# Sums of squares for the token norms: a GpSimd running sum in place of a TensorE product per row

## The chip, the cores and the metric

The kernel runs on one core of one Trainium2 chip. The metric is the device time of one execution in microseconds (us); the figure that counts is the median of several runs. One core has five engines with a queue each: TensorE (PE in the profile, its weight loads PEld), VectorE (DVE), ScalarE (ACT), GpSimd (POOL) and SyncE (SP), which here only starts DMAs. TensorE writes to PSUM, the others work mostly on SBUF.

## The reference

Two layers over 256 latent tokens and 256 context tokens of width 1024. What matters here is the norm that stands ahead of each mixer and of each mixture of experts:

```
def rms_norm(x, gain):
    xf = x.astype(jnp.float32)
    y = xf * lax.rsqrt(jnp.mean(xf * xf, axis=-1, keepdims=True) + NORM_EPS)
    return (y * gain.astype(jnp.float32)).astype(x.dtype)

for layer in range(DEPTH):
    hx = modulate(rms_norm(x, norm_mix[layer]), shift, scale)     # and hc from ctx
    ...                                                           # four mixers
    x = x + gate * (mixed @ w_out[layer])
    hx2 = modulate(rms_norm(x, norm_ffn[layer]), shift, scale)
    x = x + gate * hierarchical_moe(hx2, ...)                     # 16 experts, 2 of them per token
```

In layer 0 both streams are carried on; in layer 1 only the latent tokens are, so its second norm is over 256 tokens. All arithmetic is float32. For each token the mean of 1024 squares is needed: four times in the kernel (layer 0 mixers, layer 0 experts, layer 1 mixers, layer 1 experts).

## The kernel before, in words

The residual stream X is held in SBUF with features on partitions: eight "rows" j = 0..7 of 128 features, and for each row a tile of 128 partitions x 256 tokens per stream s (s = 0 latent, s = 1 context). A row is final once its last residual update has been added. Then `Rms.row(j)` (L349) takes over: for each stream ScalarE writes the squares into a 256-wide work tile (tag "t", six buffers), and TensorE multiplies them by `mean32`, 128 x 32 numbers of 1/1024, into one of four 32-partition strips of a PSUM bank (L354). A product in float32 stands in the trace as two records. `Rms.end` (L356) copies each bank to SBUF (ACT, tile name t<-ss), adds the four strips with products by `sel1`, one per 128 tokens (PE, ssb<-cb,t), takes the root (ACT, rtok<-ssb), inverts it (DVE), and broadcasts it back over the partitions (PE L370, then ACT rstd<-ssb). The norm proper (L377) multiplies X by rstd.

`Rms` is made and fed in four places:
- at the start of the kernel for X as loaded (L1548), two streams;
- in `out_proj` (L1000): four groups g of weight columns, each 48 products into two PSUM banks (tile pw, three buffers); then VectorE adds the rows j = 2g and 2g + 1 to X (L1020, one instruction per row and stream), and `sums.row(j)` follows at once. In layer 0 there are two streams, in layer 1 one, and there also a 32-column router product per row (tile rt);
- in the last `scatter` of layer 0's experts (L1397, called at L1486): for each row j four products (tile sct) into one of three PSUM banks, one VectorE addition per stream (L1407), `sums.row(j)`. This scatter stands behind a conditional block (L1438) that is not taken; two work tiles of tag "t" hold the placement matrices Pm until it ends.

Work that fills in around these places: the modulation products (tile ada), which run while a norm is computed, and `split_w`, which splits weights into two parts (tile wsp): a ScalarE copy, then half of the subtraction on VectorE and half on GpSimd. Weights come in 1 MB pieces through SP's queue into 22 shared slots; a DMA starts when an earlier user has given its slot back. The framework's scheduler fixes the order in each engine's queue ahead of time, by priority and its own estimates; each engine then works strictly in that order.

Helpers record most operations at one line: every product is L152, every ScalarE operation L155, every two-input elementwise operation L158, so rows of the trace are told apart by tile names.

Of the kernel before, what the change touches and what calls it, by code (L numbers as in the profile page):

```python
# [15 lines left out]
AF = mybir.ActivationFunctionType  # L16
OP = mybir.AluOpType
# [98 lines left out]
def build(tc, xT, cT, vec, cst, ada, w_in, w_out, wg, wu, wd, outT, es, dbg=None):  # L116
    nc = tc.nc
    dbg = dbg or {}
    V, S, G, T = nc.vector, nc.scalar, nc.gpsimd, nc.tensor
# [8 lines left out]
    def nm(s):  # L128
        cnt[0] += 1
        return f"{s}_{cnt[0]}"  # L130
# [6 lines left out]
    def ps(tag, shape=(512,), name="ps"):  # L137
        return psp.tile([128] + list(shape), F32, name=nm(name), tag=tag, bufs=PSB[tag])
# [3 lines left out]
    def wt(shape, tag, dt=F32, bufs=None):  # L142
        if tag in TB:
            return wk.tile([128, 516], dt, name=nm(tag), tag=tag, bufs=TB[tag])[:, :shape[0]]
        return wk.tile([128] + list(shape), dt, name=nm(tag), tag=tag, **({"bufs": bufs} if bufs else {}))
# [5 lines left out]
    def mm(out, lhsT, rhs, start, stop, **kw):  # L151
        return T.matmul(out, lhsT, rhs, start=start, stop=stop, **kw)  # L152

    def act(out, in_, f=AF.Copy, **kw):
        return S.activation(out, in_, f, **kw)  # L155

    def tt(out, a, b, op, eng=V):
        return eng.tensor_tensor(out, a, b, op=op)  # L158
# [9 lines left out]
    def load_x():  # L168
        t = [sl([8, 256], name="X") for _ in range(2)]
        for s in range(2):  # L170
            nc.sync.dma_start(t[s], xT[s])
        return lambda j, s: t[s][:, j]

    X0 = load_x()
# [5 lines left out]
    mean32 = cb[:, C_MEAN:C_MEAN + 32]  # L180
# [87 lines left out]
    def keep(n):  # L268

        live[0] = n  # L270
        issue()
# [36 lines left out]
    def ada_quad(l, q, after={}):  # L308

        pm = ps("a", name="ada")  # L310
        for k in range(KT):
            w = take('ada', l, q, k)
            M = 32 if k == 0 else 2
            for c in range(4):
                with tc.issue_after(spread[after[k]].ins) if after.get(k) in spread else nullcontext():
                    mm(pm[32 * c:32 * c + M], csil[:, k] if k else csil0[:, 0], w[:, c], k == 0, k == 7, skip_group_check=True)
            del w
            done()
            yield
        sb = wt([512], "t")  # L320
        act(sb, pm)
        pt = ps("a", name="adaT")
        for i in range(4):
            T.transpose(pt[:, 128 * i:128 * i + 128], sb[:, 128 * i:128 * i + 128], ident)
        us = slice(16 * q, 16 * q + 16)
        for s in range(2):
            tt(mods[l][:, us, s].rearrange("p (u i) -> p u i", i=4),
               pt.rearrange("p (i c r) -> p c i r", c=4, r=32)[:, :, :, s],
               (va if l + q == 0 else vs[:, l])[:, V_ADAB + 16 * q:V_ADAB + 16 * q + 16].rearrange("p (u i) -> p u i", i=4), OP.add)
        yield  # L330
# [11 lines left out]
    class Rms:  # L342


        def __init__(self, X, ns):
            self.X, self.ns = X, ns
            self.sums = [ps("m", name="ss") for _ in range(ns)]

        def row(self, j):  # L349
            g = j % 4  # L350
            for s in range(self.ns):
                sq = wt([256], "t")
                act(sq, self.X(j, s), AF.Square)
                mm(self.sums[s][32 * g:32 * g + 32, :NX], mean32, sq, j < 4, j >= 4)  # L354

        def end(self):  # L356
            n = 2 * self.ns
            pc = ps("m", [n], name="ssb")
            for s in range(self.ns):
                part = wt([256], "t")  # L360
                act(part, self.sums[s][:, :NX])
                for c in range(2):
                    mm(pc[:, 2 * s + c:2 * s + c + 1], part[:, 128 * c:128 * c + 128], sel1, s == c == 0, True,
                       skip_group_check=True)
            r = self.rtok = wt([4], "rtok", bufs=1)
            act(r[:, :n], pc, AF.Sqrt, bias=epst)
            V.reciprocal(r[:, :n], r[:, :n])
            pb = ps("m", name="ssb")
            for i in range(n):
                T.transpose(pb[:, 128 * i:128 * i + 128], r[:, i:i + 1].to_broadcast([128, 128]), ident)  # L370
            rs = []
            for s in range(self.ns):
                t = wt([256], f"rstd{s}", bufs=1)
                act(t, pb[:, NX * s:NX * s + NX])
                rs.append(t)
            return rs
# [623 lines left out]
    def out_proj(l, mh, ml, X, gate):  # L1000
        ns = 2 if l == 0 else 1
        sums = Rms(X, ns)
        sums.logits = Logits(l, X) if ns == 1 else None
        order = (2, 3, 6, 7, 0, 1, 4, 5)
        for g in range(4):
            pw = [ps("pj", name="pw") for _ in range(2)]
            hi, lo = ahead.pop(g) if g in ahead else split_w(take('out', l, g), (V, G))
            if g in AHO[l] and g < 3:
                ahead[g + 1] = split_w(take('out', l, g + 1), (V, G))
            for n_, k in enumerate(order):  # L1010
                for c in range(2):
                    cs = slice(128 * c, 128 * c + 128)
                    o = pw[c][:, :NX * ns]
                    mm(o, hi(k)[:, cs], mh(k), n_ == 0, False)
                    mm(o, hi(k)[:, cs], ml(k), False, False)
                    mm(o, lo(k)[:, cs], mh(k), False, n_ == 7)
            for c in range(2):
                j = 2 * g + c
                for s in range(ns):
                    V.scalar_tensor_tensor(X(j, s), pw[c][:, NX * s:NX * s + NX], gate[:, j, s:s + 1], X(j, s),  # L1020
                                           op0=OP.mult, op1=OP.add)
                sums.row(j)
                if sums.logits:
                    sums.logits.row(j)
        return sums
# [519 lines left out]
        plan.append(sources[key])  # L1545

    keep(LIVE[0][0])
    sums = Rms(X0, 2)  # L1548
    for j in range(8):
        sums.row(j)  # L1550
    mh, ml = mixers(0, X0, sums, first0, lambda i: (nothing(), ada_quad(0, 1), ada_quad(0, 2), nothing())[FILL[0][i]], LIVE[0])
    X = load_x()
    keep(LIVE[0][3])
    sums = out_proj(0, mh, ml, X, mods[0][:, 16:24, :])
    tap_x("x1", X)
    keep(LIVE[0][4])
    sums = moe(0, X, sums, mods[0][:, 40:48, :], ada_quad(1, 0))
# [4 lines left out]
    sums = out_proj(1, mh, ml, X, mods[1][:, 16:24, :])  # L1562
# [68 lines left out]
```

## Time and profile before

| | |
|---|---|
| median of 3 runs | 1213.12 us (1211.68 to 1213.55) |
| the profiled execution | 1214.19 us |
| its span, first to last instruction | 1212.4 us |
| PE busy | 1139.1 us, 94% |
| DVE, ACT, POOL busy | 524.8, 381.7, 189.1 us |
| from HBM | 299.29 MB |

The span is what the views cut into windows; times in them count from its start. The profiled execution lies 1.07 us above the median. In this kernel layer 0's output projection runs to about 370 us, its experts to about 697 us with the last scatter to 713 us; layer 1's output projection runs from about 929 to 963 us, its experts to the end.

### The profile page before, as it was taken

What the parts mean: (1) busy time and instruction counts of PE and PEld (TensorE: products, weight loads), DVE (VectorE), ACT (ScalarE), POOL (GpSimd) and SP (SyncE); (2) the same over time, 40 slices, a digit from 0 to 9 for tenths busy, and PEclk for the clock granted to TensorE, in tenths of its full rate; (3) what the DMA queues carried; (4) which work ended last, traced back from release to release, by engine and by line L of the source; (5) the groups of instructions that cost most, each with busy time, mean ns of one, the idle gap of its engine ahead of it and who ended that gap; (6) DMA issues with size and microseconds to landing.
All of it is one profiled execution on the core that took longest, in us unless ns stands there. A gap on an engine that the chain in (4) does not pass through costs nothing. (4 is left out here: it accounts for less than half of the span.)

```text
span 1212.4 us, 16650 instructions
## 1 busy us (share of the span) xinstructions
PE 1139.1 (94%) x6667; PEld 708.6 (58%) x6667; DVE 524.8 (43%) x1000; ACT 381.7 (31%) x648; POOL 189.1 (16%) x129
## 2 busy tenths in 40 slices
PE   5999989999998899999999789999988999999998
PEld 3699876764564453333434348975965655565654
DVE  2637658646715421322212256656887231212122
ACT  5544365533413110111000245436764221110110
POOL 1325453100302000000000012443213000000000
PEclk9999999999999899999999989999999889999999
DMA  9811016453647699898699902374245769999991
GB/s 389 330 35 70 35 36 240 177 225 123 240 177 284 273 426 426 297 387 308 211 372 426 424 7 71 139 254 163 70 174 177 288 266 402 393 388 427 425 422 39
DMA packets 44708, 303.61 MB, mean 250 GB/s; under 512 B 5456, under 2 KB 7120, under 8 KB 8784
## 3 DMA queue, kind: packets, MB, share of 16 engines
q1 hardware_dynamic: 42320, 295.52, 61.8%
q0 software_dynamic: 1296, 4.72, 1.1%
q10 hardware_dynamic: 1008, 2.22, 0.5%
q8 instruction: 56, 0.92, 0.3%
q14 instruction: 28, 0.23, 0.1%
HBM read 299.29 MB, written 3.15 MB: 249 GB/s over the span
## 5 line engine op out<-in xcount | busy, mean ns | idle before, releaser
L152 PE MATMUL pf<-hxh,wsp 128*128 128x512 f32 (+1 forms) x640 | 179.8, 365 | 9.8 <-ACT wsp L155 3.8
L152 PE MATMUL g<-w,row 128*64 128x512 f32 (+1 forms) x704 | 147.9, 595 | 2.1 <-DVE row L1335 2.1
L158 POOL TENSOR_TENSOR wsp<-w,wsp 128x1024 fp32r<-128x1024 f32 x34 | 95.1, 2800 | 334.6 <-ACT wsp L155 301.5
L152 PE MATMUL u<-w,row 128*64 128x512 f32 (+1 forms) x704 | 141.1, 592 | 0.0
L152 PE MATMUL d<-w,t 128*64 128x512 f32 (+1 forms) x704 | 137.0, 596 | 1.0 <-DVE o L1393 0.9
L152 PEld LDWEIGHTS pf<-hxh,wsp 128*128 128x128 f32 x640 | 115.2, 193 | 32.8 <-ACT wsp L155 4.7
L152 PE MATMUL pf<-hxl,wsp 128*128 128x512 f32 (+1 forms) x320 | 114.7, 360 | 1.3 <-POOL hxl L158 1.0
L152 PEld LDWEIGHTS u<-w,row 128*64 128x64 f32 (+1 forms) x704 | 55.7, 127 | 71.3 <-issue 68.9
L152 PEld LDWEIGHTS g<-w,row 128*64 128x64 f32 (+1 forms) x704 | 53.8, 127 | 74.1 <-issue 66.1
L158 DVE TENSOR_TENSOR t<-t,u 128x512 f32<-128x512 f32 x18 | 12.4, 689 | 181.9 <-PE u L152 181.9
L152 PEld LDWEIGHTS d<-w,t 128*64 128x64 f32 (+1 forms) x704 | 47.5, 126 | 73.5 <-issue 63.1
L152 PE MATMUL ptk<-wsp,hxh 128*128 128x256 f32 x480 | 90.3, 287 | 0.0
L1407 DVE SCALAR_TENSOR_TENSOR X<-sct,mods,X 128x256 f32<-128x256 f32 x112 | 50.0, 480 | 73.4 <-PE sct L152 71.5
L152 PE MATMUL sct<-t,o 128*128 128x512 f32 (+1 forms) x288 | 69.7, 368 | 10.7 <-PEq L1438 5.8
L1393 DVE SCALAR_TENSOR_TENSOR o<-d,wsl,o 128x512 fp32r<-128x512 f32 x36 | 26.3, 748 | 121.2 <-ACT o L155 120.2
L155 ACT ACTIVATE wsp<-w 128x1024 fp32r<-128x1024 f32 x72 | 73.7, 1052 | 15.9 <-POOL wsp L158 5.8
L152 PEld LDWEIGHTS ptk<-wsp,hxh 128*128 128x128 f32 x480 | 75.2, 191 | 2.3 <-issue 1.2
L152 PE MATMUL pw<-mixh,wsp 128*128 128x512 f32 (+1 forms) x256 | 67.5, 348 | 3.0 <-ACT mixh L155 3.0
L152 PEld LDWEIGHTS pf<-hxl,wsp 128*128 128x128 f32 x320 | 61.6, 193 | 11.7 <-POOL hxl L158 2.3
L152 PE MATMUL ptk<-wsp,hxl 128*128 128x256 f32 x240 | 68.2, 284 | 0.0
L152 PEld LDWEIGHTS sct<-t,o 128*128 128x128 f32 x288 | 43.9, 190 | 41.3 <-issue 26.0
L158 POOL TENSOR_TENSOR K<-K,F 64x512 f32<-64x512 f32 (+1 forms) x46 | 58.6, 1274 | 59.4 <-issue 24.1
(260 smaller groups left out, 1566.0 us busy)
## 6 DMA issues: line engine op xcount, KB each, us to landing
w<-in_wg_dram SPq DMA_DIRECT2D x64, 1024.0 KB, 8.5
w<-in_wu_dram SPq DMA_DIRECT2D x64, 1024.0 KB, 10.6
w<-in_wd_dram SPq DMA_DIRECT2D x64, 1024.0 KB, 13.1
w<-in_ada_dram SPq DMA_DIRECT2D x48, 1024.0 KB, 6.8
w<-in_w_in_dram SPq DMA_DIRECT2D x28, 1024.0 KB, 4.8
w<-in_w_out_dram SPq DMA_DIRECT2D x8, 1024.0 KB, 6.0
X<-in_xT_dram SPq DMA_DIRECT2D x4, 1024.0 KB, 4.9
hd<-hrow ACTq DMA_DIRECT2D x4, 512.0 KB, 3.6
```

What stands on the lines that cost most here:

```text
L152: return T.matmul(out, lhsT, rhs, start=start, stop=stop, **kw)
L155: return S.activation(out, in_, f, **kw)
L158: return eng.tensor_tensor(out, a, b, op=op)
L1393: V.scalar_tensor_tensor(ohl[:, 1, fs], pd[nn], w, ohl[:, 0, fs].bitcast(F32), op0=OP.mult, op1=OP.subtract)
L1407: V.scalar_tensor_tensor(X(j, s), p[:, NX * s:NX * s + NX], gate[:, j, s:s + 1], X(j, s), op0=OP.mult, op1=OP.add)
```

## The change

`Rms` gets a flag `added`, true everywhere but at the start of the kernel. With it, row 0's squares are written straight into a tile `sq[s][0]` (the buffer that later holds rstd for that stream), the squares of rows 1 to 6 are added to it by GpSimd, one addition per row and stream, and row 7's squares are kept in their own work tile. `end` multiplies both tiles by one column of `mean32`: for each stream and each 128 tokens two products accumulate in PSUM (the 128 x 128 squares are the weights, one column moves). The two PSUM banks of the strips, the copy to SBUF and the products by `sel1` fall away in the three places.

```
-    sums = Rms(X0, 2)
+    sums = Rms(X0, 2, False)
     ...
-        def __init__(self, X, ns):
-            self.X, self.ns = X, ns
-            self.sums = [ps("m", name="ss") for _ in range(ns)]
+        def __init__(self, X, ns, added=True):
+            self.X, self.ns, self.added = X, ns, added
+            if added:
+                self.sq = [[wt([256], f"rstd{s}", bufs=1)] for s in range(ns)]
+            else:
+                self.sums = [ps("m", name="ss") for _ in range(ns)]

         def row(self, j):
             g = j % 4
             for s in range(self.ns):
+                if self.added:
+                    sq = wt([256], "t") if j else self.sq[s][0]
+                    act(sq, self.X(j, s), AF.Square)
+                    if 0 < j < 7:
+                        tt(self.sq[s][0], self.sq[s][0], sq, OP.add, G)
+                    elif j:
+                        self.sq[s].append(sq)
+                    continue
                 sq = wt([256], "t")
                 act(sq, self.X(j, s), AF.Square)
                 mm(self.sums[s][32 * g:32 * g + 32, :NX], mean32, sq, j < 4, j >= 4)
     ...
             for s in range(self.ns):
+                if self.added:
+                    for c in range(2):
+                        for i in range(2):
+                            mm(pc[:, 2 * s + c:2 * s + c + 1], self.sq[s][i][:, 128 * c:128 * c + 128], mean32[:, 0:1],
+                               s == c == i == 0, True, skip_group_check=True)
+                    del self.sq[s][:]
+                    continue
                 part = wt([256], "t")
                 act(part, self.sums[s][:, :NX])
                 ...
```

## Rows read from the trace of the kernel before

**Rows 1.** Busy time by stage: window, its length, then each engine's busy us (instructions).
```profile
331.00:372.00 41.00, 41.00 (x183) 27.60 (x184) 6.30 (x16) 6.38 (x16) 0.00 (x0) 1.00 0.51 190
690.00:722.00 32.00, 22.97 (x112) 10.20 (x111) 12.48 (x28) 14.92 (x30) 4.72 (x2) 0.88 0.24 100
...
1100.00:1212.40 112.40, 102.82 (x558) 62.27 (x554) 24.96 (x53) 11.27 (x18) 0.00 (x0) 1.00 0.77 320
```

**Rows 2.** SP's waits from 960 to 1165 us: in total, times, longest.
```profile
SPq L265 <- PE d L152: 68.9, 12, 13.5
SPq L265 <- DMA w<-in_wg_dram: 3.8, 3, 1.6
```

**Rows 3.** Timeline of PE, layer 0's output projection, around one group's end.
```profile
342.27 0.61 PE L152 MATMUL pw<-mixh,wsp 128*128 128x512 f32 x2
342.72 0.39 PE L152 MATMUL pw<-mixl,wsp 128*128 128x512 f32 x1
343.04 0.62 PE L152 MATMUL ss<-t,cb 128*32 128x256 f32 x2
343.59 0.73 PE L152 MATMUL pw<-mixh,wsp 128*128 128x512 f32 x2
```

**Rows 4.** Timeline of DVE, the same projection: the additions behind groups 2, 3, 4.
```profile
342.01 1.66 DVE L1020 SCALAR_TENSOR_TENSOR X<-pw,mods,X 128x256 f32<-128x256 f32 x4 [9.69 <-PE pw L152]
355.95 1.66 DVE L1020 SCALAR_TENSOR_TENSOR X<-pw,mods,X 128x256 f32<-128x256 f32 x4 [12.27 <-PE pw L152]
369.11 1.66 DVE L1020 SCALAR_TENSOR_TENSOR X<-pw,mods,X 128x256 f32<-128x256 f32 x4 [11.50 <-PE pw L152]
```

**Rows 5.** Timeline behind that projection, from the last squares to the root.
```profile
369.62 1.65 ACT L155 ACTIVATE t<-X 128x256 f32<-128x256 f32 x4 [11.51 <-DVE X L1020]
...
373.26 0.97 PEld L152 LDWEIGHTS ssb<-cb,t 128*128 128x128 f32 x8 [0.86 <-ACT t L155]
374.36 0.26 ACT L155 ACTIVATE rtok<-ssb,epst 128x4 f32<-128x4 f32 x1 [1.46 <-PE ssb L152]
```

**Rows 6.** GpSimd's forms of two-input operation in the whole span: count, busy, mean ns.
```profile
L158 POOL TENSOR_TENSOR wsp<-w,wsp 128x1024 fp32r<-128x1024 f32 x34 | 95.1, 2800 | 334.6 <-ACT wsp L155 301.5 <-issue 22.0 <-PE sc L152 8.0
L158 POOL TENSOR_TENSOR t<-X,rstd 128x256 f32<-128x256 f32 x8 | 6.8, 875 | 47.8 <-ACT rstd L155 47.3 <-ACT H L155 0.2
```

**Rows 7.** The same operation by tile: ns least, median, most.
```profile
L158 POOL TENSOR_TENSOR t<-X,rstd x8: 730/909/1009, 376.6 to 382.9; 128x256 f32<-128x256 f32 x8
```

**Rows 8.** Timeline of layer 0's last scatter and the norm behind it.
```profile
696.98 1.62 PE L152 MATMUL sct<-t,o 128*128 128x512 f32 x3 [5.83 <-PEq L1438]
698.30 0.87 ACT L155 ACTIVATE t<-X 128x256 f32<-128x256 f32 x2 [4.26 <-DVE X L1407]
705.05 2.39 POOL L158 TENSOR_TENSOR wsp<-w,wsp 128x1024 fp32r<-128x1024 f32 x1 [8.59 <-ACT wsp L155]
...
718.22 0.26 ACT L155 ACTIVATE rtok<-ssb,epst 128x4 f32<-128x4 f32 x1 [1.87 <-PE ssb L152]
722.10 1.65 PE L152 MATMUL pf<-hxh,wsp 128*128 128x512 f32 x3 [2.64 <-ACT hxh L155]
```

**Rows 9.** Busy time of the instructions on tile ss alone, by window.
```profile
939.00:962.10 23.10, 3.27 (x12) 1.08 (x12) 0.00 (x0) 0.00 (x0) 0.93 0.68 277
```

**Rows 10.** Timeline behind layer 1's output projection.
```profile
962.68 0.81 ACT L155 ACTIVATE t<-X 128x256 f32<-128x256 f32 x2 [6.89 <-DVE X L1020]
965.33 0.26 ACT L155 ACTIVATE rtok<-ssb,epst 128x2 f32<-128x2 f32 x1 [0.42 <-PE ssb L152]
```

**Rows 11.** Busy time by stage, as rows 1; the last three columns are granted clock, DMA share, GB/s.
```profile
697.00:712.00 15.00, 15.00 (x54) 6.39 (x58) 7.77 (x15) 6.80 (x14) 2.39 (x1) 0.89 0.04 17
722.00:728.00 6.00, 5.90 (x14) 4.43 (x15) 5.33 (x11) 3.72 (x8) 2.64 (x2) 0.53 0.00 0
```

**Rows 12.** Products of the modulation between 697 and 722 us: count, then ns least, median, most.
```profile
L152 PE MATMUL ada<-w,csil x40: 592/592/617, 711.6 to 716.6; 128*2 128x512 f32 x32, 128*32 128x512 f32 x8
```

**Rows 13.** Timeline of PE at the low clock, start of layer 1's first projection.
```profile
724.12 0.63 PE L152 MATMUL pf<-hxh,wsp 128*128 128x512 f32 x1
724.54 0.63 PE L152 MATMUL pf<-hxl,wsp 128*128 128x512 f32 x1
```

## The prediction

> **What bounds the kernel now.** I read the table of busy time by stage first. Through layer 0's output projection TensorE is busy in 41.00 of 41 us, and in the last 112 us in 102.82 [rows 1]: TensorE bounds nearly everything. DMA comes close in the experts (0.77 of all engines over the last stage), so the waits of SP's queue are next: from 960 to 1165 us it waited 68.9 us for TensorE's products on d to give slots back, and 3.8 us for transfers of wg [rows 2]. The weights follow TensorE and not the other way round, so time saved on TensorE ahead of the experts moves their stream with it. The exception is the stretch from 690 to 722 us, 22.97 us busy of 32 at a granted clock of 0.88 [rows 1]: there a chain over several engines decides. Three places change: A, layer 0's output projection; B, layer 0's last scatter; C, layer 1's output projection. Each has a running part, where products of squares stand among other products, and a tail from the last square to the root.
>
> **A, running part.** Removed from it: 12 products by mean32 (the other four stand in the tail). The timeline shows what one costs beside pw: pw at 342.72, the product at 343.04, pw again at 343.59 [rows 3]. That is 0.87 us between two pw products. Undisturbed, two of them take 0.45 us, from 342.27 to 342.72 [rows 3], about 0.227 each; 48 make 10.9 us. Check it on whole groups: VectorE's additions behind groups 2, 3 and 4 start at 342.01, 355.95 and 369.11 [rows 4], so two groups take 13.94 and 13.16 us, 3.0 and 2.3 us over 10.9. In group 3 four products stand singly, which makes 0.75 us each, as the timeline shows with the stretched pw behind it; in group 4 three stand together. The first boundary has the pattern of the last, 2.3. Sum 7.6 us. In exchange there is nothing on TensorE. GpSimd's additions are hidden: it has no instruction in this stage [rows 1], and has over ten us per group for two rows. What could be late next is VectorE's release of a PSUM bank at each boundary, 0.2 to 0.3 us, so I take 7.0 (bounds 5.5 and 7.6).
>
> **A, tail.** Before: the four squares end at 369.62 + 1.65 = 371.27, then come products, a copy and the products ssb; the root starts at 374.36 [rows 5]. After: the last additions are those of row 6, whose squares end after the first and second of four, at 370.04 and 370.45. GpSimd's 128 x 256 form takes 875 ns in the mean [rows 6], between 730 and 1009 [rows 7]; the second addition ends at 371.5 to 372.1. Then four more products of N = 1 are due; today's four are 8 records in 0.97 us [rows 5], and there are eight after the change, the first stream's half during the additions. Root at 372.8 to 373.2: a gain of 1.2 to 1.6, I take 1.3. If the scheduler puts all eight behind the last addition, 0.4 is left; if an addition costs 1.9 it is a loss of about 0.7. Bounds -0.7 and 1.6.
>
> **B.** Here the scatter's 16 products by mean32 stand between sct products and pace the chain: root at 718.22, first projection product at 722.10 [rows 8], 3.9 us later. After the change GpSimd is the slowest: row 1's first square ends at 698.30 + 0.43 [rows 8], twelve additions at 0.875 + 0.05 for a handover (estimate) make 11.1, and one subtraction on wsp (2.39) may fall between them [rows 8]: 698.7 + 11.1 + 2.4 = 712.2. The last products add 1.0: root at 713.2, gain 5.0. What else stands there, two copies and a table load on ScalarE, falls away or lies under the additions. Queued behind the additions on GpSimd is that subtraction, for the layer's second column group, which is due only after the first group's products. Of the six work tiles two are held, so ScalarE's squares run at GpSimd's pace; behind them in its queue are two weight copies with the same late due time. Lower bound: additions at 1.009 with gaps of 0.08 put the root at 715.2, gain 3.0. Upper bound: additions at 0.73 without the subtraction would allow more than TensorE does. It has some 26 sct products, 8 of them at half clock at 0.42 [rows 13] and the others at 0.23, together 7.6 us, and 40 records of modulation at about 0.11 (their starts from 711.6 to 716.6 cover them with others, [rows 12]), 4.6, and 2.0 for the new products: done at 711.2, gain 7.0.
>
> **C.** Running part: the mean32 products take 3.27 us in 12 records, that is six products [rows 9], some next to router products that need the same change of shape anyway. I take 2.8 (bounds 2.0 and 3.3). Tail: squares end at 963.09 and 963.49, root at 965.33 [rows 10]. After: one addition, 963.1 to 964.0, four products of 8 records at 0.97 us, root at 965.0: gain 0.3 (bounds -0.7, addition at 1.9, and 0.7).
>
> **Sum.** 7.0 + 1.3 + 5.0 + 2.8 + 0.3 = 16.4 us off the profiled execution's 1214.19, so 1197.8; it stood 1.07 above the median, so the median is 1196.7. All lower bounds give 9.1 us (1204), all upper ones 20.2 (1193). The new order that the scheduler finds elsewhere I allow 3 us either way: own range 1190 to 1207.
>
> **Rivals.** [...]
>
> Second, the weight stream decides. If DMA and not TensorE ends the experts, time saved ahead of them is waited out there: 1213, no change. For it, DMA's share of 0.77 in the last stage [rows 1]; against it, SP's queue waits for TensorE [rows 2].
>
> Third, the other side: GpSimd's additions are far dearer than the profiled form, because each needs the result of the one two before it, a pattern that no row shows. Fifteen additions stand on a path that decides (twelve in B, two in A's tail, one in C's). At 0.93 the gain is 16.4; it is gone at 0.93 + 16.4 / 15 = 2.0 us, and at 2.8, the mean of the form four times as wide [rows 6], the kernel takes 28 us more than forecast, 1225. Against: the very form ran eight times at 1009 ns or less, beside VectorE work of the same kind [rows 7].
>
> The change could also fail to do what it says: the scheduler can put the new products, which wait for GpSimd, early in TensorE's queue, with modulation products behind them. In B that puts up to 4.6 us of modulation behind the root, hidden in part by the 3.9 us to the first projection product; 1199 to 1201, inside my range.
>
> **How the numbers follow.** Forecast (with its misordered form) 0.66; clock 0.14; weights 0.07; dear additions 0.05; more than 22 us gained, by a better order elsewhere, 0.05; an unlucky order elsewhere, about 1214 to 1217, 0.03. About 0.2% (2.4 us) is what a measurement of this kernel can tell from no change. Faster by more than that: 0.66 + 0.14 + 0.05 and a little of the weights' case, 0.87. Within it: 0.06. Slower: 0.07. The range reaches over the clock's case and both bounds: 1189 to 1208.
>
> **What would show it.** In A the additions L1020 stand 10.9 to 11.2 us apart, and no ss record is left behind the start of the kernel. GpSimd shows 12 additions of 128 x 256 in A and in B and 6 in C, at 0.73 to 1.0 us. B's root comes about 15 to 16.5 us after the first sct product behind the conditional block, against 21.2. From each norm to the next place the distances stay as before. The prediction is wrong if the additions take over 1.3 us, if sct runs at 0.42 throughout, or if TensorE waits for weights in the experts.

## Result, and the profile after

| | before | after |
|---|---|---|
| median | 1213.34 us (1211.68 to 1214.02, 4 runs) | 1199.2 us (1197.09 to 1201.26, 4 runs) |
| the profiled execution | 1214.19 us | 1197.09 us |
| its span | 1212.4 us | 1195.2 us |
| PE, DVE, ACT, POOL busy | 1139.1, 524.8, 381.7, 189.1 us | 1122.9, 526.6, 379.7, 211.6 us |

The ratio is 0.9885, with the interval 0.9864 to 0.9907: 14.1 us faster. The forecast was 1196.7, 2.5 us too low; the measured median lies inside its range of 1189 to 1208. The profiled execution of before lies above all four of its runs, that of after is the fastest of its four: the two traces differ by 17.1 us, 3 us more than the medians. So the ladder below, made from the traces, shows where the time went, and the runs of the experiments have to say how much of it is real.

The ladder takes the same event in both traces and lists after minus before; the last column is what was gained between this event and the one above it.

| event | before | after | difference | gained |
|---|---|---|---|---|
| A: addition behind the first group | 330.66 | 330.75 | +0.09 | -0.1 |
| A: addition behind the fourth group | 369.11 | 361.83 | -7.28 | 7.4 |
| A: root | 374.36 | 366.81 | -7.55 | 0.3 |
| first sct product behind the conditional block | 696.98 | 689.88 | -7.10 | -0.5 |
| B: root | 718.22 | 703.63 | -14.59 | 7.5 |
| C: addition behind the first group | 940.46 | 924.79 | -15.67 | 1.1 |
| C: addition behind the last group | 962.17 | 945.37 | -16.80 | 1.1 |
| C: root | 965.33 | 948.65 | -16.68 | -0.1 |
| layer 1's experts: first product on g | 979.01 | 962.35 | -16.66 | 0.0 |
| end of the span | 1212.4 | 1195.2 | -17.2 | 0.5 |

The stages first: busy time in windows of the kernel after, for A, for B and behind it, and for the start of C: length, busy us of PE, PEld, DVE, ACT and POOL (instructions), granted clock of TensorE, DMA share, GB/s.

```profile
331.00:363.00 32.00, 32.00 (x140) 25.55 (x138) 5.90 (x15) 5.37 (x14) 7.13 (x11) 1.00 0.61 222
690.00:704.00 14.00, 13.59 (x79) 8.31 (x79) 9.43 (x17) 9.01 (x18) 12.30 (x13) 0.86 0.05 22
704.00:708.00 4.00, 1.14 (x5) 0.74 (x5) 2.32 (x8) 1.97 (x5) 0.34 (x2) 0.52 0.00 0
708.00:712.00 4.00, 4.00 (x11) 2.95 (x12) 3.76 (x8) 2.66 (x5) 1.98 (x2) 0.63 0.00 0
...
925.00:927.00 2.00, 2.00 (x6) 0.78 (x5) 1.13 (x3) 1.25 (x3) 0.72 (x1) 0.50 1.00 418
927.00:929.00 2.00, 2.00 (x7) 1.15 (x7) 0.00 (x0) 0.00 (x0) 0.72 (x1) 0.50 0.99 418
929.00:931.00 2.00, 2.00 (x17) 2.00 (x16) 0.00 (x0) 0.00 (x0) 0.00 (x0) 0.89 1.03 426
```

A still keeps TensorE busy throughout (32.00 of 32), as in [rows 1], and GpSimd works beside it for 7.13 us, where it did nothing. B's 14 us from the skipped block to the root hold 13.59 us of TensorE and 12.30 us of GpSimd: both are nearly full. Behind the root TensorE is busy for 1.14 us of four, and the granted clock is 0.52 and 0.63 in the mean of these two stretches; [rows 11] have 0.53 from the first projection product on. The last three rows belong to C and are taken up below.

What TensorE's work gave back in A is in VectorE's additions behind groups 2, 3 and 4 (timeline of after; start, length, operation, in brackets the idle time before it and what ended it).

```profile
340.03 1.66 DVE L1039 SCALAR_TENSOR_TENSOR X<-pw,mods,X 128x256 f32<-128x256 f32 x4 [7.62 <-PE pw L152]
350.93 1.66 DVE L1039 SCALAR_TENSOR_TENSOR X<-pw,mods,X 128x256 f32<-128x256 f32 x4 [9.24 <-PE pw L152]
361.83 1.66 DVE L1039 SCALAR_TENSOR_TENSOR X<-pw,mods,X 128x256 f32<-128x256 f32 x4 [9.24 <-PE pw L152]
```

They stand 10.90 and 10.90 us apart, where [rows 4] have 13.94 and 13.16: exactly 48 undisturbed pw products of 0.227 us. The tail behind them, to the root:

```profile
362.41 1.59 ACT L155 ACTIVATE t<-X 128x256 f32<-128x256 f32 x4 [9.31 <-DVE X L1039]
362.96 1.41 POOL L158 TENSOR_TENSOR rstd<-rstd,t 128x256 f32<-128x256 f32 x2 [8.07 <-ACT t L155]
363.75 0.38 PE L152 MATMUL ssb<-cb,rstd 128*128 128x1 f32 x2 [0.30 <-POOL rstd L158]
364.06 1.06 PE L152 MATMUL ada<-w,csil 128*32 128x512 f32 x8
365.05 0.38 PE L152 MATMUL ssb<-cb,t 128*128 128x1 f32 x2
...
366.81 0.27 ACT L155 ACTIVATE rtok<-ssb,epst 128x4 f32<-128x4 f32 x1 [2.81 <-PE ssb L152]
```

The two additions end at 364.37, 2.54 us behind the start of the last VectorE addition. The root is another 2.44 us later, because eight records of modulation (ada, 1.06 us) stand between the new products in TensorE's queue, and seven of the eight new products run only behind them.

B in the timeline of after, from the skipped block to the first projection product:

```profile
689.88 7.40 PE L152 MATMUL sct<-t,o 128*128 128x512 f32 x23 [5.68 <-PEq L1457]
691.70 10.33 POOL L158 TENSOR_TENSOR rstd<-rstd,t 128x256 f32<-128x256 f32 x12 [2.24 <-ACT t L155]
697.22 4.50 PE L152 MATMUL ada<-w,csil 128*32 128x512 f32 x40
...
701.65 0.38 PE L152 MATMUL ssb<-cb,rstd 128*128 128x1 f32 x2
702.00 2.34 POOL L158 TENSOR_TENSOR wsp<-w,wsp 128x1024 fp32r<-128x1024 f32 x1
...
702.56 0.36 PE L152 MATMUL ssb<-cb,rstd 128*128 128x1 f32 x2
...
703.63 0.27 ACT L155 ACTIVATE rtok<-ssb,epst 128x4 f32<-128x4 f32 x1 [2.82 <-PE ssb L152]
707.97 1.65 PE L152 MATMUL pf<-hxh,wsp 128*128 128x512 f32 x3 [2.70 <-ACT hxh L155]
```

The root comes 13.75 us behind the first sct product, 21.24 before [rows 8]. Twelve additions ran in one stretch of 10.33 us, 0.86 each, and the subtraction on wsp (2.34) stands behind all of them. TensorE's modulation ends at 701.72, GpSimd's additions at 702.03: the two engines finish nearly together. Which of them sets the root shows in TensorE's windows from the first sct product to the start of the modulation, to the first new product and to the root (columns as above):

```profile
689.88:697.22 7.34, 7.34 (x24) 5.58 (x24) 5.17 (x12) 5.22 (x12) 5.52 (x8) 0.73 0.12 48
697.22:701.65 4.43, 4.43 (x42) 1.00 (x41) 4.18 (x5) 3.52 (x6) 4.43 (x5) 1.00 0.01 4
701.65:703.63 1.98, 1.94 (x20) 1.86 (x16) 0.00 (x0) 0.00 (x0) 1.98 (x2) 1.00 0.00 0
```

TensorE is busy throughout, and no bracket, so no wait, stands at a product on rstd. The first product on the context stream's sum starts at 702.56, half a microsecond behind the end of the last addition (0.3 in the trace of the changed kernel again). So TensorE's own work sets the root here, and GpSimd is ready just ahead of it.

GpSimd's additions over the whole span of after (count, busy us, mean ns), which answer to [rows 6 and 7]:

```profile
L158 POOL TENSOR_TENSOR rstd<-rstd,t 128x256 f32<-128x256 f32 x30 | 23.2, 807 | 49.3 <-ACT t L155 49.2
```

SP's waits from 943 to 1148 us of after answer to [rows 2]; the weights still follow TensorE:

```profile
SPq L265 <- PE d L152: 68.7, 12, 13.5
...
SPq L265 <- DMA w<-in_wg_dram: 3.3, 4, 1.3
```

### The profile page after: what moved, and what is told of

It reads as the page before. It is cut to its first block, busy times and chain, and to the rows that moved or that the text cites. A ratio compares the mean times of both kernels' runs of the same rounds, so it can differ in the third digit from the quotient of the medians.

```text
span 1195.2 us, 16587 instructions
## 1 busy us (share of the span) xinstructions
PE 1122.9 (94%) x6607; PEld 706.5 (59%) x6607; DVE 526.6 (44%) x1000; ACT 379.7 (32%) x643; POOL 211.6 (18%) x159
## 5 line engine op out<-in xcount | busy, mean ns | idle before, releaser
L158 DVE TENSOR_TENSOR t<-t,u 128x512 f32<-128x512 f32 x18 | 12.4, 688 | 181.9 <-PE u L152 181.9
```

## Experiments

All kernels below start from the changed one. Medians of before lie between 1212.99 and 1213.71 in the three groups of runs, and the ratios are to those. Numbers of places are from each run's own trace.

**The changed kernel again**, unedited, beside the three that follow.

> The changed kernel again, for a pair with the parts. Theory (each place gives what its own trace shows and the gain is carried to the end): 14 to 16 us under the kernel before. Rival (the 17 us between the two profiled executions are the true size and the medians of four runs fell badly): 16.5 to 17.5 us.

Measured: 1199.35 us (1198.98 to 1200.29), ratio 0.9886 (0.9871 to 0.9902): 13.9 us, just under what was expected. This is the value that the others are set against.

**One place at a time.** Three kernels keep the additions in one place and go back to the 32-column products in the other two.

```
A only:  -        sums = Rms(X, ns)                                 # out_proj
         +        sums = Rms(X, ns, l == 0)
         -        sums = Rms(X, ns) if l + 1 < DEPTH else None      # the experts
         +        sums = Rms(X, ns, False) if l + 1 < DEPTH else None
B only:  +        sums = Rms(X, ns, False)                          # out_proj
C only:  +        sums = Rms(X, ns, l == 1)                         # out_proj
         +        sums = Rms(X, ns, False) if l + 1 < DEPTH else None
```

> GpSimd sums in layer 0's output projection alone; the other places as before. Theory: 7.0 to 7.6 us gained, nearly all of it between the additions to X (10.9 us apart instead of 13.2 to 13.9), the tail between -0.3 and +0.3, and the same distance left at the end. Rival (the weight stream of the experts behind it swallows time saved ahead of it): under 3 us at the end, with TensorE waiting for weights in layer 0's experts.

> GpSimd sums in the last scatter of layer 0's experts alone. Theory: root 13.7 us behind the first product after the conditional block instead of 21.2, so 6.5 to 7.5 us gained at the end. Rival (TensorE at half clock in the scatter takes the gain): 0 to 2 us. Rival (the 7.5 us are partly an effect of A's other order of products): 4 to 5 us.

> GpSimd sums in layer 1's output projection alone. Theory: 2.4 to 3.1 us as predicted, if the granted clock comes up as early behind that projection's wait as in the kernel before (about 943 us on its scale). Rival (only 1 us, as the changed kernel's trace shows from the first addition to the root, because the router products keep the change of shape and the tail waits for GpSimd): 0.8 to 1.4 us whatever the clock does.

Measured: A alone 1210.46, ratio 0.9974 (0.9965 to 0.9983), -2.8 us; B alone 1209.51, 0.9972 (0.9961 to 0.9983), -3.8; C alone 1215.9, 1.0021 (1.0012 to 1.003), 2.6 us slower. All three expectations missed, and together the parts make -4.0 us where the whole makes -13.9. The traces say where: up to layer 1's experts the parts do add up. At the first product on g there, A alone is 5.96 us ahead of before, B alone 8.91, C alone 1.18, in sum 16.05, against 16.66 and 15.15 in the two traces of the whole. The loss is in the last 10 us. Timeline of TensorE at the end of the kernel with A alone:

```profile
1196.56 0.63 PE L152 MATMUL sct<-t,o 128*128 128x256 f32 x3
1197.34 0.63 PE L152 MATMUL sct<-t,o 128*128 128x256 f32 x3 [0.16 <-DVE o L1412]
1201.53 4.13 PE L152 MATMUL sct<-t,o 128*128 128x256 f32 x20 [3.56 <-PEq L1457]
```

and the same in the trace of before, for which no row stands above:

```profile
1202.56 0.62 PE L152 MATMUL sct<-t,o 128*128 128x256 f32 x3
1203.34 0.62 PE L152 MATMUL sct<-t,o 128*128 128x256 f32 x3 [0.16 <-DVE o L1393]
1205.06 2.63 PE L152 MATMUL sct<-t,o 128*128 128x256 f32 x20 [1.10 <-DVE X L1407]
```

Behind layer 1's conditional block, which is skipped, TensorE with A alone waits 3.56 us for its own sequencer (PEq), and the 20 products behind take 4.13 us instead of 2.63. With B alone the wait is 3.69 us, with C alone 3.44; before and in both traces of the changed kernel there is none. None of the three edits touches this block or anything near it.

**A theory for the lost 3 us: where the code lies.** What differs is how many instructions stand ahead of the block in TensorE's compiled program. In the compiled programs the branch that skips it (304 instructions further on) stands at instruction 14055 before and 13933 in the changed kernel (no wait), at 14005, 14006 and 14032 with one part (wait). In the stretch from 3.5 to 1.0 us ahead of the products behind the block, each of the traces with the wait has one load of instructions (queue q8, 0.02 MB), and none of six traces without the wait has any. (The rows stand with the third kernel below.) Which positions bring the wait was an estimate of the author's, fitted to these five values, so three new ones were predicted: one-column products at the very start of the kernel, where TensorE waits 8.9 us for a transfer (tile cb) in the trace of after, shift all later code by two instructions each.

```
+    pad = ps("a", name="pad")
+    for _ in range(30):                       # 43 in the third kernel
+        mm(pad[:, 0:1], ones, ones[:, 0:1], True, True)
```

Layer 1's block is the one in question in all three: A alone with 30 of them (branch at 14065), C alone with 30 (14092), and the whole change with 43 (14019), where the estimate puts the wait back.

> The kernel with GpSimd sums in layer 0's output projection alone, with 30 products of one column put in at the very start, while TensorE waits for its first transfer; they compute nothing that is used and move the later TensorE program by 60 instructions. Theory (the parts fell short of their places because the skip over layer 1's conditional block then waits about 3.5 us for code, depending only on where in the program the branch stands): the wait of TensorE's sequencer behind that block goes, the end comes 4 us earlier than without the shift, 6 to 7.5 us under the kernel before. Rival (A's gain is really lost in the experts): 2 to 3.5 us under the kernel before, as without the shift.

> The kernel with GpSimd sums in layer 1's output projection alone, shifted by the same 60 instructions. Theory (code position): 4 us earlier than without the shift, so 0.7 to 2.5 us under the kernel before. Rival (C alone is a loss): 2 to 3 us over the kernel before, as without the shift.

> [...] Theory (code position): a wait of 3.4 to 3.6 us behind that block and TensorE at half clock after it, 3.5 to 4.5 us over the changed kernel, 1203 to 1204 us. Rival (the wait came with the parts' own order of work): no wait, within 1 us of the changed kernel.

Measured: A alone, shifted: 1207.74, ratio 0.995 (0.9936 to 0.9963), -6.0 us instead of -2.8, no wait. C alone, shifted: 1213.24, 0.9997 (0.9988 to 1.0006), -0.5 instead of +2.6, which can't be told from no change, no wait. The whole change, shifted to a bad place: 1201.93, 0.991 (0.9895 to 0.9925), 2.6 us above the changed kernel, wait back. Its rows at the end:

```profile
1188.11 0.62 PE L152 MATMUL sct<-t,o 128*128 128x256 f32 x3 [0.17 <-DVE o L1415]
1192.31 4.13 PE L152 MATMUL sct<-t,o 128*128 128x256 f32 x20 [3.58 <-PEq L1460]
```

and those of A alone, shifted:

```profile
1194.39 0.63 PE L152 MATMUL sct<-t,o 128*128 128x256 f32 x3 [0.16 <-DVE o L1415]
1196.10 2.62 PE L152 MATMUL sct<-t,o 128*128 128x256 f32 x20 [1.08 <-DVE X L1429]
```

The instruction loads (queue, kind: packets, MB, share) from 3.5 to 1.0 us ahead of the 20 products, first with the whole change shifted, where the wait is (1188.81 to 1191.31),

```profile
q8 instruction: 1, 0.02, 3.0%
```

then all that moves in the trace of after, where it is not (1184.88 to 1187.38):

```profile
DMA packets 0, 0.00 MB, mean 0 GB/s; under 512 B 0, under 2 KB 0, under 8 KB 0
```

The waits came out as the theory said, two removed and one made, by an edit that does no work of the kernel; the sizes came out less well, C's above all. From layer 1's first product on g to the end of the span the traces take 233.4 us before, 232.9 and 233.1 changed, 233.5 and 233.0 with A or C shifted, and 236.8, 236.8, 236.1 and 236.3 in the four with the wait. Each kernel set against the runs of before beside it, the wait costs 3.2 us for A, 3.1 for C and 2.1 for the whole (2.6 to 2.7 if the medians are subtracted as they stand), less than the 4 us expected of A and C and the 3.5 to 4.5 of the third. That the position decides is shown: the four with the wait stand from 14005 to 14032, the four without at 13933 and from 14055 to 14092, and two more among the kernels below, 13884 (the start of the kernel too) and 13973 (row 6 not added), have none either. That a load of instructions lies inside the wait is shown as well, with A alone and with the whole change shifted 2.8 us ahead of the 20 products. That TensorE waits for this load is not, for the traces without the wait have one of the same size close by (0.3 to 0.6 us ahead of the products in after, 0.2 to 0.5 behind their start in before); nor is shown what makes a position a bad one.

With the wait out, the parts are 6.0 for A, 0.5 for C, and for B 3.8 plus the 2.1 to 3.2 of the others (an estimate, not run): 5.9 to 7.0. The sum of 12.4 to 13.5 stands against 13.9 for the whole.

**The additions twice.** GpSimd runs each addition also into a scratch tile that nobody reads.

```
                     if 0 < j < 7:
+                        tt(wt([256], "scr", bufs=1), self.sq[s][0], sq, OP.add, G)
                         tt(self.sq[s][0], self.sq[s][0], sq, OP.add, G)
```

> The changed kernel with every GpSimd addition run twice, once into a scratch tile. Theory (GpSimd paces the last scatter): twelve more additions of 0.81 to 0.88 us put B's root 9.7 to 10.5 us later; A's tail gets 0.8 to 1.6 later, C's 0.8; together 11 to 13 us over the changed kernel, about back at the kernel before. Rival (TensorE's own work paces the scatter, GpSimd is hidden under it): under 4 us over the changed kernel.

Measured: 1211.01, ratio 0.998 (0.9969 to 0.9991), 11.7 us above the changed kernel. Root in B 26.0 us behind the first sct product (718.91 against 692.89). GpSimd in B in this trace, shortened:

```profile
694.71 0.74 POOL L158 TENSOR_TENSOR scr<-rstd,t 128x256 f32<-128x256 f32 x1 [2.20 <-ACT t L155]
695.52 0.74 POOL L158 TENSOR_TENSOR rstd<-rstd,t 128x256 f32<-128x256 f32 x1
...
706.29 2.34 POOL L158 TENSOR_TENSOR wsp<-w,wsp 128x1024 fp32r<-128x1024 f32 x1
...
716.00 0.73 POOL L158 TENSOR_TENSOR rstd<-rstd,t 128x256 f32<-128x256 f32 x1
```

From 694.71 to 716.73 GpSimd has no gap to speak of. Less the subtraction, which now falls among them, that is 19.7 us for 24 additions, 0.82 each. TensorE, which waits for no sum in B in the trace of after, now does:

```profile
715.30 0.59 PE L152 MATMUL ssb<-cb,rstd 128*128 128x1 f32 x2 [10.80 <-POOL rstd L158]
```

Of the 12.3 us by which the root is later, 11.7 are GpSimd's longer stretch, and 0.6 lie behind it, where the new products stand 0.43 us apart instead of 0.22, at a granted clock of 0.50. A's tail is 0.3 us longer and C's 0.5, less than expected. So once GpSimd is the slower engine in B, its additions count in full. Who was the slower one in the changed kernel this run can't tell: twelve more additions are far more than the half microsecond between the two.

**The additions on VectorE**, all of them, or those of stream 0 alone.

```
-                        tt(self.sq[s][0], self.sq[s][0], sq, OP.add, G)
+                        tt(self.sq[s][0], self.sq[s][0], sq, OP.add, V)             # all
+                        tt(self.sq[s][0], self.sq[s][0], sq, OP.add, G if s else V) # stream 0
```

> The changed kernel with the 30 additions on VectorE at 0.42 us. Theory: in B VectorE's 14 additions to X, 12 sums and 2 weight subtractions are 6.7 + 5.0 + 2.4 to 3.3 us, so the last sum comes at about the same time as GpSimd's did, or up to 1 us earlier; A's tail 0.5 us shorter; together 0 to 1.5 us under the changed kernel. Rival (VectorE's queue holds the additions to X back, and TensorE's PSUM banks with them): 2 to 5 us over the changed kernel.

> The changed kernel with latent sums on VectorE and context sums on GpSimd. Theory: in B GpSimd has six additions and ends 5 us earlier, but the new products then wait for the modulation products, which end at the same time as GpSimd's last addition does in the changed kernel; so 0 to 1 us gained in B, 0.5 in A's tail, 0.3 in C's. Rival (GpSimd alone set B's end): 4 to 5 us under the changed kernel.

Measured: 1199.77, ratio 0.9888 (0.9871 to 0.9904), and 1199.2, 0.9874 (0.9857 to 0.9891): no difference from the changed kernel. VectorE's addition is far shorter (groups of the first of the two; count, busy us, mean ns):

```profile
L158 DVE TENSOR_TENSOR rstd<-rstd,t 128x256 f32<-128x256 f32 x30 | 13.6, 482 | 1.4 <-ACT t L155 0.9
```

and the root in B still stands 14.75 and 14.6 us behind the first sct product, a little later than the 13.75 and 13.5 of the two traces with GpSimd. In both traces TensorE works from the first sct product to the root without waiting for a sum. So GpSimd does not set B's end in the changed kernel: shorter additions gain nothing there. Why TensorE's own work takes a microsecond more was not settled. In A nothing is lost between the groups: with all additions on VectorE its additions to X behind groups 2, 3 and 4 start at 340.01, 350.91 and 361.81, 10.90 us apart as in the trace of after. Only the tail is longer, from the first of the last additions to X to the root 5.4 us instead of 5.0, where 0.5 less was expected; C's is 0.7 shorter.

**Row 6 not added.** Row 6's squares are kept as row 7's are, and three products instead of two take them up, so that no addition stands on the tails.

```
-                    if 0 < j < 7:
+                    if 0 < j < 6:
...
-                        for i in range(2):
+                        for i in range(3):
```

> The changed kernel with row 6's squares kept as they are, like row 7's: 10 additions on GpSimd in A and B and 5 in C, and three products instead of two per stream and 128 tokens at the end. Theory (the tails wait for GpSimd for only 0.3 to 0.7 us, and in B TensorE's modulation products end with the additions): A's tail -0.3 to +0.5, B -0.5 to +0.7, C's tail 0 to -0.4, together within 1 us of the changed kernel. Rival (GpSimd alone sets the tails): 1.7 us gained in B and 0.7 to 1.5 in the other tails, 2.5 to 3.5 us under the changed kernel.

Measured: 1200.33, ratio 0.9888 (0.9873 to 0.9903), 1.0 us above the changed kernel. From A's last VectorE addition to its root it takes 0.4 us more than in the changed kernel, from C's 0.2 us less: one GpSimd addition less and the additional products about cancel. In B GpSimd ends its additions 9.05 us behind the first sct product, in the trace of after 12.15, and the root comes no earlier: it stands 15.4 us behind that product, 1.6 us later than there, outside what was expected. The 23 sct products take 8.14 us in place of 7.40, at a granted clock of 0.82 over the whole stretch instead of 0.86. At the end of this trace TensorE stands still for 1.3 us among the 20 sct products, which the others do not show:

```profile
1194.45 0.86 PE L152 MATMUL sct<-t,o 128*128 128x256 f32 x5 [1.10 <-DVE X L1426]
1196.60 2.91 PE L152 MATMUL sct<-t,o 128*128 128x256 f32 x15 [1.29 <-issue]
```

The branch of this kernel stands at 13973, between 13933 without the wait and 14005 with it. Whether the pause comes from that was not tested.

**The start of the kernel too.** `Rms` with additions also for X as loaded.

```
-    sums = Rms(X0, 2, False)
+    sums = Rms(X0, 2)
```

> The changed kernel with GpSimd sums at the start of the kernel too, where the products of squares stand beside little other TensorE work. Theory (a gain needs other products beside them, or a chain that they pace): the first norm's root, at about 17.5 us, gets later, by 12 additions of 0.8 us that begin with the second row's square against 16 products that end at 15 us: 2 to 5 us slower than the changed kernel. Rival (removing 32-column products gains wherever they stand): 1 to 3 us faster.

Measured: 1204.01, ratio 0.9922 (0.9904 to 0.9939), 4.7 us above the changed kernel, 4.1 of them already at the start of layer 0's output projection (its first pw product at 314.87 instead of 310.81). In the first 30 us TensorE is busy for 16.10 us even with the 32-column products, so there was little to give back there, and with the additions it waits 3.2 us for GpSimd's sums.

## Why the prediction was right, and where it was off

The two main steps of the argument held: what was taken off TensorE was gained, and the weights followed it. The rivals fell. The weights' wait stayed as it was (68.7 us of SP's queue for d, 3.3 for wg). The additions took 0.81 us in the mean and stood 0.86 apart in B, where 0.93 was taken, far below the break-even of 2.0. And B was not lost to the clock, to which the forecast gave 0.14 and over which its range reaches. No run shows B's gain lost to it: the gain of 7.5 us came at a granted clock of 0.86 over B's 14 us, the sct products took 7.34 us at 0.73, and the low stretch around the block (0.50) lasts 6.8 us in both traces.

**A, running part**: forecast 7.0, the traces show 7.4. The count of 12 products between pw products and their price were right. The 0.2 to 0.3 us per boundary for VectorE's release of a bank, which no row gave, no run shows either: the additions stand 10.90 us apart.

**A, tail**: forecast 1.3, shown 0.3. The GpSimd part was right: the second addition ended 2.54 us behind the start of the last VectorE addition, forecast 2.4 to 3.0. The step that failed is "the first stream's half during the additions": only one of its four products ran there, eight modulation records were put behind it, and from the last addition to the root it took 2.44 us in place of 1.1 to 1.3. That is nearly the case priced at 0.4 in the forecast.

**B**: forecast 5.0 with 7.0 as upper bound, shown 7.5, and 7.75 in the trace of B alone. The root's 13.75 us behind the first sct product lie outside the 15 to 16.5 that the forecast gave as its sign. The step that failed is "After the change GpSimd is the slowest". In the trace of after TensorE works without a wait from the first sct product to the root, so the sum that the forecast had only as its upper bound is the one that happened: sct products 7.34 us (7.6 in the forecast), modulation 4.43 (4.6), new products 1.98 (2.0). GpSimd stayed just ahead of it because two of its terms were put too high: an addition with its handover takes 0.86 us, not 0.925, which is 0.8 us over twelve, and the subtraction, of which the forecast said that it "may fall between them", stood behind all of them, 2.4 us. The runs bear this out from both sides: with GpSimd's work doubled TensorE waits 10.80 us for it, and with additions on VectorE, or two fewer of them, the root comes no earlier.

**C**: forecast 3.1, shown 1.0, and 0.5 in the medians with C alone and shifted, which is not clear of noise. This is a term that was mis-sized. Part of it is the clock. TensorE waits 3.0 us for mixh ahead of the first group, and from about the end of that wait on windows of 1 us show a granted clock of 0.50 for a while; the length of this low stretch is estimated from them as the sum of (1 - clock) / 0.5. The traces show it in two lengths (before and after are left out of the table, because there it began 1 to 2 us ahead of the first addition):

| kernels | low stretch | first to last addition in C |
|---|---|---|
| C with 32-column products: A alone, B alone, A alone shifted | 3.4 us | 22.26, 22.39, 22.29 |
| C with additions: twice, on VectorE, one stream each | 3.4 us | 19.46, 19.98, 19.98 |
| C with additions: changed again, C alone, C alone shifted, changed shifted, row 6 unadded, start too | 6.8 us | 21.63, 21.53, 21.49, 21.56, 21.64, 21.48 |

With equal low stretches the products that fell away are worth 2.3 to 2.4 us (leaving aside the 19.46, where it too began earlier), inside the bounds of 2.0 to 3.3 and below the 2.8 taken. Why they are not worth the whole 2.8 was not tested. With the longer one 0.6 to 0.9 us is left. In the trace of after it runs from 922.6 to 929.4 us, over both router boundaries (0.50, 0.50 and 0.89 in the windows above). The forecast weighed the clock for B alone; it mattered in C. What makes the low stretch the shorter or the longer one was not settled: taking the mean32 products out goes with the longer one in 6 of 9 kernels, the three kernels that keep them all have the shorter one, and the three others differ only in what GpSimd and VectorE do. C's tail gave nothing (-0.1, forecast 0.3).

**Elsewhere.** The trace of before was itself slow in one stretch: from B's first projection product to C's first addition it takes 0.8 to 1.5 us more than every other trace, also than those of A alone and A alone shifted (1.1 and 0.9), which have the 32-column products at both ends. So about 1 us of the 17.1 between the two profiled executions is not the change's. In sum the forecast erred by +2.1 in C and +1.0 in A's tail, and by -2.5 in B and -0.4 in A, as the traces have them. That these nearly cancel is luck: 16.4 forecast, 16.1 in the three places of the traces, 13.9 to 14.1 in the medians. Why the medians show some 2 us less than the places was not settled; executions of one kernel differ by up to 4 us (1197.09 to 1201.26).

## What to carry to other kernels

Count what a small odd-shaped product costs among large ones by the spacing of its neighbours: in A 12 products of 32 columns cost 7.4 us, and moving them to an engine that was idle there returned all of it. When an engine takes over a serial chain, look at what finishes last: here twelve additions on GpSimd were ready half a microsecond before TensorE used them, so making them shorter gained nothing, and doubling them put the root 12.3 us later. And when parts of a change do not add up, look in the trace for a wait that has nothing to do with any of them before a theory on the parts is made.

## What the runs showed of the hardware that was not expected

- A skipped conditional block can cost TensorE 3.4 to 3.7 us of waiting for its sequencer, and slower products behind it (20 in 4.13 us instead of 2.63), or nothing at all, according to how many instructions stand ahead of it: 30 one-column products more at the start of the kernel took it away, 43 brought it on. That is 2.1 to 3.2 us in the medians, more than the effect of C. Layer 0's block, a longer skip (583 instructions against 304), cost such a wait of 5.7 to 5.9 us, in the trace of before as in those of the changed kernel.
- In C, from about the end of a wait of 3.0 us on, the granted clock was 0.50 for 3.4 us in some kernels and for 6.8 in others, with nearly the same work on TensorE; between kernels with additions that is worth 1.6 us.
- GpSimd's 128 x 256 addition took 0.81 us in the mean in a chain of which each needs the one two before, less than the 0.875 of the unchained form before: waiting on itself costs it nothing that the rows show.
